# One more FFN pair as a Strassen group, half of the first weight sums added by transfers, and one pass of the down projection per block

## The chip, the core and the metric

The kernel runs on one core of one Trainium2 chip. The metric is the device time of one execution in microseconds (us), the median of several runs. PE is the matmul engine (TensorE), DVE is VectorE, ACT is ScalarE, POOL is GpSimd and SP is SyncE, which here only issues transfers. PEld in a view is the loading of a matmul's stationary operand, which overlaps the matmul before it.

## What is computed

One block of a streaming encoder on 256 frames of width 2048, all in float32: a half-step SwiGLU FFN, two token mixers side by side (chunked attention and retention), a second half-step FFN and a last norm.

```python
def swiglu_ffn(x, w_gate, w_up, w_down):
    return (jax.nn.silu(x @ w_gate) * (x @ w_up)) @ w_down

x = x + 0.5 * swiglu_ffn(rmsnorm(x, norm_ffn1_g[l]), ffn1_w_gate[l], ffn1_w_up[l], ffn1_w_down[l])
h = rmsnorm(x, norm_mix_g[l]); proj = h @ w_in[l]     # 2048 x 11264, then attention, retention, gates
x = x + merged @ w_out[l]
x = x + 0.5 * swiglu_ffn(rmsnorm(x, norm_ffn2_g[l]), ffn2_w_gate[l], ffn2_w_up[l], ffn2_w_down[l])
return rmsnorm(x, norm_final_g)
```

The hidden width of an FFN is 5632, which is 11 blocks of 512 columns. Each block needs a pair of products, x by 512 columns of w_gate and x by the same 512 columns of w_up, and then 512 rows of w_down.

## The kernel before

**Products.** A float32 operand is split into hi (rounded to the matmul's float32r type, a cast on ACT, line L126) and lo (the rest, a subtraction on DVE, line L127). A product is three matmuls (`three`, lines L137, L138, L140): hi by hi, lo of the activations by hi of the weights, hi of the activations by lo of the weights. The activations stand transposed, 128 by 128, and the weights run past them 512 columns at a time, so every matmul of the list is 128x512.

**Steps.** The whole program is one list of steps. A step uses one weight tile of 2 by 128 rows by 512 columns (512 KB). A standard step serves both 128-frame tiles with it: 12 matmuls. `run` walks the list; for each step it issues the steps' loads (SP queue, 5 buffers `raw`), prepares weights up to four steps ahead (`prep`, 4 buffers each of hi and lo) and then issues the step's matmuls. What a job's end hands out (copies, gates, norms) is put some steps later by `later`. Every engine works its own instructions in the order in which they were issued.

**Strassen groups.** `Strassen` computes the pair of products of one block with 7 half-size products in place of 8. Its weight quarters are: k, the upper half of the w_up rows (tiles `z..k`, four of them, jc 0 to 3), x, the upper half of the w_gate rows (tiles `z..x`), and the two lower halves, which arrive as `raw` tiles. k and x are loaded by POOL's queue, eight transfers of 512 KB into a ring of 30 tiles that activations and gates use too. A group (named z and a step number, such as z243) has four phases of half-size steps, 6 matmuls each; `r` steps use a loaded quarter and `s` steps use a sum:

- phase 0: `00r 01r 00s 02r 01s 03r 02s 03s`. The r steps split k and then add k to x on DVE (`first`, line L528); the s steps split that sum.
- phase 1: the r steps split a raw tile and add it to x (L583); the s steps split x, then x minus k goes to k (L570) and a POOL transfer with `accum_op=add` adds another quarter of w_up to x straight from memory (`third`, line L571).
- phase 2: raw tiles and the new k. Phase 3: the four x tiles.

Products run on sums of the activations that were prepared once. At the end of phases, `end` copies and combines the partial results.

**Which pairs.** Of 11 blocks per FFN, nine are groups and two (`PLAIN = (9, 10)`) are done as standard jobs of 8 steps for gate and 8 for up. The five wide pairs of the mixers' input projection are groups too.

**Down.** `down` multiplies the hidden blocks by w_down in passes: a pass takes one or two blocks and runs four jobs, one for each 512 columns of the result. All passes but the last add to x in place: a job's two PSUM banks are seeded with twice x (ACT, L775), the products are added, and half of the bank is copied back (ACT, L778). Passes are `((9, 0), (1, 2), (10, 3), (4, 5), (6,), (7,), (8,))`.

**Weaving.** `weave` mixes the standard steps (plain pairs and down) into the groups: after each pair of group steps it earns `rate * SHARE[i]`, and a standard step goes in when enough is earned and its inputs are at hand. The last pass and six steps more are kept for the end of the FFN.

Of the kernel before, what the change touches and what calls it, by code (L numbers as in the profile page):

```python
# [72 lines left out]
def block_kernel(ctx: ExitStack, tc: tile.TileContext, x, g1, w1g, w1u, w1d, gm, w_in, rel, woa, wor, wo,  # L73
# [439 lines left out]
    class Strassen:  # L513
# [1 line left out]

        def __init__(self, norm, w1, col1, w2, col2, evict):
# [15 lines left out]
        def loads(self):  # L534


            def go(tiles, i, jc):
                tiles[jc] = apool.tile([P, KC, NB], F32, tag="act", name=f"{self.name}{'kx'[i]}{jc}")
                nc.gpsimd.dma_start(tiles[jc], chunk(self.w[i], self.rows(0, jc), self.col[i]))

            return [
                lambda tiles=tiles, i=i, jc=jc: go(tiles, i, jc)
                for jc in range(HALF_K // KC) for i, tiles in enumerate((self.kept, self.x))
            ]

        def steps(self):

# [9 lines left out]
        def step(self, phase, jc, of_sum):  # L557
            made = {}
            name = f"{self.name}{phase}{jc}{'rs'[of_sum]}"
            n = HALF_K // KC  # L560

            def load():
                made["raw"] = weights_tile(f"raw{name}")
                i = 2 - phase
                fetch(made["raw"], self.w[i], self.rows(1, jc), self.col[i])

            def third():

# [24 lines left out]
            bank, form, fresh, closing = {  # L593
# [4 lines left out]
            }[phase, of_sum]  # L598
# [68 lines left out]

        return done

    def weave(jobs, apart, groups, lead, start=None):  # L670


        queue = [(job, k) for job in jobs for k in range(0, job.nk, KC)]
# [14 lines left out]

        for _ in range(lead):
            next_standard()  # L690
        rate = (len(queue) - apart) / (len(groups) * sum(SHARE))
        credit = 0.0
        first = len(steps) - 8
        for n, (b, make) in enumerate(groups.items()):
            group = make()
            loads = group.loads()
            if start is not None and n == 0:
                loads[0] = lambda load=loads[0]: [start(), load()]
            kept.extend((first + i if n == 0 else 0, fn) for i, fn in enumerate(loads))
            for i, part in enumerate(group.steps()):  # L700
                steps.extend(part)
                credit += rate * SHARE[i]
                if i + 1 == len(SHARE):
# [8 lines left out]
    def ffn(name, norm, wg, wu, wd, after, start=None):  # L712
# [10 lines left out]
        def plain(b):  # L723
            gates = {}

            wait = GATE_WAIT if start is not None and b == PLAIN[0] else 0

            def gate_done(acc):
                def go():
# [20 lines left out]
        def paired(b):  # L750
            got = {}

            def evict(t, side, r):
                if side == 1:
                    nc.scalar.activation(r, r, AF.Silu)
                    got[t] = r
                    return
                nc.vector.scalar_tensor_tensor(got[t], r, norm.scale(t), got[t], op0=ALU.mult, op1=ALU.mult)
                if t == 1:
                    later(4, lambda: put_mid(b, got))  # L760

            return Strassen(norm, wu, b * NB, wg, b * NB, evict)

        def down(blocks, last):

# [30 lines left out]
        groups = {b: (lambda b=b: paired(b)) for b in range(nblocks) if b not in PLAIN}  # L796
        weave(jobs, len(downs[PASSES[-1]]) * len(PASSES[-1]) * 4 // KC + HELD, groups, LEAD, start)


    n1 = Norm("n1", gains[:, 0, :], True)  # L800
# [221 lines left out]
    def gates(col1, col2, func, dsts):  # L1022
# [22 lines left out]
        0, groups, MIX_LEAD,  # L1045
    )
    mixed = len(steps)
    add([proj(VR + NB, nat_done("vr", 1, AF.Copy))])
# [209 lines left out]
```

## Time and profile before

| | |
|---|---|
| runs | 2064.11 us median of 3 (2062.82 to 2065.65) |
| profiled execution | span 2061.4 us, the only time it has |
| PE, DVE, ACT, POOL busy | 2045.3, 1754.4, 1402.9, 273.3 us |
| transfers | 473.28 MB, 230 GB/s on average |
| first FFN, mixers, second FFN | up to about 700 us, to about 1360 us, to the end |
| one group of the first FFN (z243) with what is woven in | 454.35 to 520.52 us |

The median of the runs is 2.7 us above the span of the profiled execution. A view by windows gives, for each stretch, the busy time of each engine with the count of its instructions, the granted clock of PE and the mean busy share of the 16 DMA engines (a share a little above 1 comes from packets that end outside of the window). A matmul's own duration in the rows (0.39 us) includes the pipeline; the distance between two starts is what one costs.

### The profile page before, as it was taken

What the parts mean: (1) busy time and instruction counts of PE and PEld (TensorE: products, weight loads), DVE (VectorE), ACT (ScalarE), POOL (GpSimd) and SP (SyncE); (2) the same over time, 40 slices, a digit from 0 to 9 for tenths busy, and PEclk for the clock granted to TensorE, in tenths of its full rate; (3) what the DMA queues carried; (4) which work ended last, traced back from release to release, by engine and by line L of the source; (5) the groups of instructions that cost most, each with busy time, mean ns of one, the idle gap of its engine ahead of it and who ended that gap; (6) DMA issues with size and microseconds to landing.
All of it is one profiled execution on the core that took longest, in us unless ns stands there. A gap on an engine that the chain in (4) does not pass through costs nothing.

```text
span 2061.4 us, 26148 instructions
## 1 busy us (share of the span) xinstructions
PE 2045.3 (99%) x9256; PEld 1691.9 (82%) x9256; DVE 1754.4 (85%) x1824; ACT 1402.9 (68%) x1732; POOL 273.3 (13%) x322
## 2 busy tenths in 40 slices
PE   9999999999999999999999999999999999999998
PEld 7788888888888888888888888888888878888886
DVE  7998899899997799899966667568989988998986
ACT  7677667777777767776665434556776677677785
POOL 1111211122111110122100000010122012110200
PEclk9999999999999999999999999999999999999999
DMA  8776876788678777788775645575787668876873
GB/s 308 207 225 230 269 227 207 239 264 258 191 231 258 240 205 251 258 284 260 227 267 175 223 143 187 187 245 170 235 273 234 200 224 273 240 206 233 281 215 133
DMA packets 219315, 473.28 MB, mean 230 GB/s; under 512 B 14816, under 2 KB 15568, under 8 KB 219184
## 3 DMA queue, kind: packets, MB, share of 16 engines
q1 hardware_dynamic: 161088, 309.89, 44.7%
q0 software_dynamic: 54752, 155.88, 27.9%
q10 hardware_dynamic: 3344, 5.84, 0.8%
q8 instruction: 72, 1.18, 0.2%
q14 instruction: 59, 0.48, 0.1%
HBM read 462.65 MB, written 8.91 MB: 229 GB/s over the span
## 4 chain that ended last, share of the span: by engine, by line
PE 93%; DVE 3%; DMA 2%; ACT 1%; issue 1%; SPq 0%; DVEq 0%; POOLq 0%; POOL 0%; ACTq 0%
PE acc L140 17%; PE acc L137 17%; PE acc L138 17%; DMA raw<-in_ffn_w_down_dram 2%; DVE lo L127 1%; ACT hi L126 0%; PE z684a L140 0%; PE z380a L137 0%; PE z953a L138 0%; PE z684a L138 0%; PE z418a L137 0%; PE z723a L138 0%; PE z380a L140 0%; PE z281a L138 0%; PE z723a L137 0%
## 5 line engine op out<-in xcount | busy, mean ns | idle before, releaser
L127 DVE TENSOR_TENSOR lo<-raw,hi 128x1024 fp32r<-128x1024 f32 x399 | 487.1, 1224 | 179.1 <-ACT hi L126 174.3
L126 ACT CAST hi<-raw 128x1024 fp32r<-128x1024 f32 x399 | 417.7, 1050 | 226.8 <-PE acc L138 143.7
L775 ACT ACTIVATE acc<-xall 128x512 f32<-128x512 f32 x96 | 57.5, 599 | 8.0 <-DVE f1g L742 3.6
L778 ACT ACTIVATE xall<-acc 128x512 f32<-128x512 f32 x96 | 56.6, 589 | 9.2 <-PE acc L140 7.4
L137 PE MATMUL acc<-hi,mgh 128*128 128x512 f32 x128 | 50.2, 392 | 0.0
L138 PE MATMUL acc<-hi,mgl 128*128 128x512 f32 x128 | 49.9, 390 | 0.0
L137 PE MATMUL acc<-hi,nma01h 128*128 128x512 f32 x96 | 38.7, 403 | 0.0
L137 PE MATMUL acc<-hi,nma00h 128*128 128x512 f32 x96 | 38.6, 402 | 0.0
L138 PE MATMUL acc<-hi,nma00l 128*128 128x512 f32 x96 | 37.5, 391 | 0.0
L137 PE MATMUL acc<-hi,nma10h 128*128 128x512 f32 x96 | 37.5, 391 | 0.0
L138 PE MATMUL acc<-hi,nma01l 128*128 128x512 f32 x96 | 37.5, 390 | 0.0
L138 PE MATMUL acc<-hi,nma11l 128*128 128x512 f32 x96 | 37.5, 390 | 0.0
L137 PE MATMUL acc<-hi,nma11h 128*128 128x512 f32 x96 | 37.4, 390 | 0.0
L138 PE MATMUL acc<-hi,nma10l 128*128 128x512 f32 x96 | 37.4, 390 | 0.0
L140 PE MATMUL acc<-lo,mgh 128*128 128x512 f32 x128 | 35.6, 390 | 0.0
L140 PE MATMUL acc<-lo,nma01h 128*128 128x512 f32 x96 | 29.6, 390 | 0.0
L140 PE MATMUL acc<-lo,nma00h 128*128 128x512 f32 x96 | 29.6, 390 | 0.0
L140 PE MATMUL acc<-lo,nma11h 128*128 128x512 f32 x96 | 29.6, 390 | 0.0
L140 PE MATMUL acc<-lo,nma10h 128*128 128x512 f32 x96 | 29.6, 390 | 0.0
L140 PEld LDWEIGHTS acc<-lo,mgh 128*128 128x128 f32 x128 | 24.0, 188 | 5.0
L137 PEld LDWEIGHTS acc<-hi,mgh 128*128 128x128 f32 x128 | 24.1, 188 | 4.9
L138 PEld LDWEIGHTS acc<-hi,mgl 128*128 128x128 f32 x128 | 24.1, 188 | 4.8
(6130 smaller groups left out, 6933.7 us busy)
## 6 DMA issues: line engine op xcount, KB each, us to landing
raw<-in_ffn_w_down_dram SPq DMA_DIRECT2D x176, 512.0 KB, 6.1
raw<-in_w_in_dram SPq DMA_DIRECT2D x96, 512.0 KB, 4.7
raw<-in_ffn_w_up_dram SPq DMA_DIRECT2D x32, 512.0 KB, 10.2
raw<-in_w_out_dram SPq DMA_DIRECT2D x32, 512.0 KB, 4.0
raw<-in_ffn_w_gate_dram SPq DMA_DIRECT2D x31, 512.0 KB, 5.9
raw<-in_w_out_att_dram SPq DMA_DIRECT2D x16, 512.0 KB, 4.3
raw<-in_w_out_ret_dram SPq DMA_DIRECT2D x16, 512.0 KB, 4.0
z380x<-in_w_in_dram POOLq DMA_DIRECT2D x8, 512.0 KB, 7.4
```

The source lines that it names most:

```text
L126: nc.scalar.copy(hi, raw)
L127: nc.vector.tensor_sub(lo, raw, hi.bitcast(F32))
L137: nc.tensor.matmul(acc, ahi, whi, start=first, stop=False, **more)
L138: nc.tensor.matmul(acc, alo, whi, start=False, stop=False, **more)
L140: nc.tensor.matmul(acc, ahi, wlo, start=False, stop=last, **more)
L775: nc.scalar.activation(acc, xs[t][:, cols], AF.Copy, scale=2.0)
L778: nc.scalar.activation(xs[t][:, cols], acc, AF.Copy, scale=0.5)
```

## The change

Three things change, in both FFNs; the mixers keep their shares under the name `MIX_SHARE`.

1. Block 9 becomes a group too: ten of eleven pairs are groups, and only block 10 is plain.
2. For two of the four x tiles of each FFN group (`ADDED = (2, 3)`), the sum x + k is no longer made by DVE. After the last of the eight loads, POOL issues two transfers that read k's quarter of w_up from memory again and add it to x. Groups of the mixers keep the sums on DVE.
3. Every pass of down takes a single block: `((10,), (0,), (1,), ... (9,))`. `SHARE` is another table: fewer standard steps in phase 0 and phase 2, more in phase 1.

```diff
-SHARE = (0.85,) * 4 + (1.0,) * 4 + (0.8,) + (0.4,) * 3 + (0.15,) * 4
-PLAIN = (9, 10)
-PASSES = ((9, 0), (1, 2), (10, 3), (4, 5), (6,), (7,), (8,))
+MIX_SHARE = (0.85,) * 4 + (1.0,) * 4 + (0.8,) + (0.4,) * 3 + (0.15,) * 4
+SHARE = (0.7,) * 2 + (0.2,) * 2 + (1.3,) * 4 + (0.3,) * 4 + (0.2,) * 4
+ADDED = (2, 3)
+PLAIN = 10
+PASSES = ((10,),) + tuple((b,) for b in range(10))
...
+            def add_on():
+                for jc in self.added:
+                    nc.gpsimd.dma_start(self.x[jc], chunk(self.w[0], self.rows(0, jc), self.col[0]), accum_op=ALU.add)
...
+            out[-1] = lambda last=out[-1]: [last(), add_on()]
...
                     if phase == 0:
                         made["w"] = split(self.kept[jc], name)
-                        self.first(jc)
+                        if jc not in self.added:
+                            self.first(jc)
...
-            return Strassen(norm, wu, b * NB, wg, b * NB, evict)
+            return Strassen(norm, wu, b * NB, wg, b * NB, evict, ADDED)
...
-        first, second = [plain(b) for b in PLAIN]
-        order = [first, second[:1], downs[PASSES[0]], second[1:]] + [downs[p] for p in PASSES[1:]]
-        jobs = [job for part in order for job in part]
+        jobs = plain(PLAIN) + [job for p in PASSES for job in downs[p]]
```

In the changed kernel these lines stand a little lower: L126 and L127 are L128 and L129, `first` is L531, the loads L542, the added transfers L546, `third` L580, seeding and copying back L785 and L788.

**POOL's queue.** Before, for the group z243: the last of its eight loads, then the four accumulating transfers of phase 1. A name with in_ffn1_w_up is w_up, with w_gate w_gate.

```order
L539 DMA z243k2_3860<-in_ffn1_w_up_dram 128x2x512
L539 DMA z243x2_3873<-in_ffn1_w_gate_dram 128x2x512
L539 DMA z243k3_3887<-in_ffn1_w_up_dram 128x2x512
L539 DMA z243x3_3905<-in_ffn1_w_gate_dram 128x2x512
L571 DMA z243x0_3776<-in_ffn1_w_up_dram 128x2x512
L571 DMA z243x1_3830<-in_ffn1_w_up_dram 128x2x512
L571 DMA z243x2_3873<-in_ffn1_w_up_dram 128x2x512
L571 DMA z243x3_3905<-in_ffn1_w_up_dram 128x2x512
```

After, for z263, the group at the same place:

```order
L542 DMA z263k2_4140<-in_ffn1_w_up_dram 128x2x512
L542 DMA z263x2_4153<-in_ffn1_w_gate_dram 128x2x512
L542 DMA z263k3_4167<-in_ffn1_w_up_dram 128x2x512
L542 DMA z263x3_4185<-in_ffn1_w_gate_dram 128x2x512
L546 DMA z263x2_4153<-in_ffn1_w_up_dram 128x2x512
L546 DMA z263x3_4185<-in_ffn1_w_up_dram 128x2x512
L580 DMA z263x0_4050<-in_ffn1_w_up_dram 128x2x512
L580 DMA z263x1_4104<-in_ffn1_w_up_dram 128x2x512
L580 DMA z263x2_4153<-in_ffn1_w_up_dram 128x2x512
L580 DMA z263x3_4185<-in_ffn1_w_up_dram 128x2x512
```

Two transfers (L546) stand behind the last load. The first waits for the landing of the load of x2, the second for that of x3. In the program before, the load into x3 waits until the tile that it takes over was split in phase 3 of the group ahead (31s); in the changed one the ring of 30 tiles has more free tiles, and that load waits for the split of 21s, in the middle of phase 2. The last group of the second FFN waits for 23s.

**DVE, phase 0.** Before, z243; a name `lo` with a number alone is the split of a standard step:

```order
L127 TENSOR_TENSOR loz24300r_3915<-z243k0_3750,hiz24300r_3914 128x1024
L528 TENSOR_TENSOR z243x0_3776<-z243x0_3776,z243k0_3750 128x1024
L127 TENSOR_TENSOR loz24301r_3927<-z243k1_3818,hiz24301r_3926 128x1024
L528 TENSOR_TENSOR z243x1_3830<-z243x1_3830,z243k1_3818 128x1024
L127 TENSOR_TENSOR loz24300s_3938<-z243x0_3776,hiz24300s_3937 128x1024
L127 TENSOR_TENSOR loz24302r_3948<-z243k2_3860,hiz24302r_3947 128x1024
L528 TENSOR_TENSOR z243x2_3873<-z243x2_3873,z243k2_3860 128x1024
L758 SCALAR_TENSOR_TENSOR z205c22_3881<-z205a_3401,n1rstd_88,z205c22_3881 128x512
L127 TENSOR_TENSOR lo247_3961<-raw247_3726,hi247_3960 128x1024
L127 TENSOR_TENSOR loz24301s_3973<-z243x1_3830,hiz24301s_3972 128x1024
L127 TENSOR_TENSOR loz24303r_3984<-z243k3_3887,hiz24303r_3983 128x1024
L528 TENSOR_TENSOR z243x3_3905<-z243x3_3905,z243k3_3887 128x1024
```

After, z263:

```order
L129 TENSOR_TENSOR loz26300r_4197<-z263k0_4024,hiz26300r_4196 128x1024
L531 TENSOR_TENSOR z263x0_4050<-z263x0_4050,z263k0_4024 128x1024
L129 TENSOR_TENSOR loz26301r_4209<-z263k1_4092,hiz26301r_4208 128x1024
L531 TENSOR_TENSOR z263x1_4104<-z263x1_4104,z263k1_4092 128x1024
L129 TENSOR_TENSOR loz26300s_4220<-z263x0_4050,hiz26300s_4219 128x1024
L129 TENSOR_TENSOR loz26302r_4230<-z263k2_4140,hiz26302r_4229 128x1024
L768 SCALAR_TENSOR_TENSOR z227c22_4161<-z227a_3706,n1rstd_88,z227c22_4161 128x512
L129 TENSOR_TENSOR lo267_4242<-raw267_4000,hi267_4241 128x1024
L129 TENSOR_TENSOR loz26301s_4254<-z263x1_4104,hiz26301s_4253 128x1024
L129 TENSOR_TENSOR loz26303r_4265<-z263k3_4167,hiz26303r_4264 128x1024
L129 TENSOR_TENSOR loz26302s_4275<-z263x2_4153,hiz26302s_4274 128x1024
```

The sums into x2 and x3 (L528 before) are gone, and one split of a standard step has left this stretch.

**ACT, the end of phase 1 and the start of phase 2.** Before, z243, from the change of one down job to the next (L775 seeds, L778 copies back) on:

```order
L775 ACTIVATE acc28_0_4206<-xall_77 128x512
L778 ACTIVATE xall_77<-acc26_0_4028 128x512
L775 ACTIVATE acc29_1_4209<-xall_77 128x512
L778 ACTIVATE xall_77<-acc27_1_4031 128x512
L126 CAST hiz24312s_4212<-z243x2_3873 128x1024
L126 CAST hiz24313s_4224<-z243x3_3905 128x1024
L126 CAST hi265_4236<-raw265_4106 128x1024
L126 CAST hiz24320r_4254<-rawz24320r_4137 128x1024
L126 CAST hiz24321r_4266<-rawz24321r_4149 128x1024
L629 ACTIVATE z243c12_4278<-z243a_3953,n1minus_89 128x512
L126 CAST hi268_4280<-raw268_4180 128x1024
L126 CAST hiz24320s_4298<-z243k0_3750 128x1024
```

After, z263:

```order
L785 ACTIVATE acc56_0_4450<-xall_77 128x512
L788 ACTIVATE xall_77<-acc54_0_4306 128x512
L785 ACTIVATE acc57_1_4453<-xall_77 128x512
L788 ACTIVATE xall_77<-acc55_1_4309 128x512
L128 CAST hiz26312s_4456<-z263x2_4153 128x1024
L128 CAST hiz26313s_4468<-z263x3_4185 128x1024
L128 CAST hi283_4480<-raw283_4354 128x1024
L128 CAST hiz26320r_4498<-rawz26320r_4381 128x1024
L128 CAST hiz26321r_4510<-rawz26321r_4393 128x1024
L639 ACTIVATE z263c12_4522<-z263a_4234,n1minus_89 128x512
L128 CAST hi286_4524<-raw286_4424 128x1024
L785 ACTIVATE acc58_0_4542<-xall_77 128x512
```

A down job now has two steps and not four, so the next four instructions of seeding and copying back come eight instructions later; before, none stands in the rows shown. In all there are 64 more seeds and 64 more copies back.

More of the change, by code (lines that the diff above doesn't have):

```diff
@@ L513, in block_kernel, with __init__ @@
     class Strassen:
-        def __init__(self, norm, w1, col1, w2, col2, evict):
+        def __init__(self, norm, w1, col1, w2, col2, evict, added=()):
+            self.added = added
             self.norm, self.w, self.col, self.evict = norm, (w1, w2), (col1, col2), evict
@@ L539, in go @@
                 nc.gpsimd.dma_start(tiles[jc], chunk(self.w[i], self.rows(0, jc), self.col[i]))
-            return [
+            def add_on():
+                for jc in self.added:
+                    nc.gpsimd.dma_start(self.x[jc], chunk(self.w[0], self.rows(0, jc), self.col[0]), accum_op=ALU.add)
+            out = [
                 lambda tiles=tiles, i=i, jc=jc: go(tiles, i, jc)
@@ L544, in loads @@
             ]
+            out[-1] = lambda last=out[-1]: [last(), add_on()]
+            return out
         def steps(self):
@@ L668, in x_updated, with weave @@
         return done
-    def weave(jobs, apart, groups, lead, start=None):
+    def weave(jobs, apart, groups, lead, share, start=None):
         queue = [(job, k) for job in jobs for k in range(0, job.nk, KC)]
@@ L690, in weave @@
             next_standard()
-        rate = (len(queue) - apart) / (len(groups) * sum(SHARE))
+        rate = (len(queue) - apart) / (len(groups) * sum(share))
         credit = 0.0
@@ L701, in weave @@
                 steps.extend(part)
-                credit += rate * SHARE[i]
-                if i + 1 == len(SHARE):
+                credit += rate * share[i]
+                if i + 1 == len(share):
                     at_hand[b] = len(steps) + 7
@@ L724, in plain @@
             gates = {}
-            wait = GATE_WAIT if start is not None and b == PLAIN[0] else 0
+            wait = GATE_WAIT if start is not None and b == PLAIN else 0
             def gate_done(acc):
@@ L790, in ffn @@
         downs = {blocks: down(blocks, blocks is PASSES[-1]) for blocks in PASSES}
-        first, second = [plain(b) for b in PLAIN]
-        order = [first, second[:1], downs[PASSES[0]], second[1:]] + [downs[p] for p in PASSES[1:]]
-        jobs = [job for part in order for job in part]
+        jobs = plain(PLAIN) + [job for p in PASSES for job in downs[p]]
         for job, follow in zip(jobs, jobs[1:]):
             job.next = follow
-        groups = {b: (lambda b=b: paired(b)) for b in range(nblocks) if b not in PLAIN}
-        weave(jobs, len(downs[PASSES[-1]]) * len(PASSES[-1]) * 4 // KC + HELD, groups, LEAD, start)
+        groups = {b: (lambda b=b: paired(b)) for b in range(nblocks) if b != PLAIN}
+        weave(jobs, len(downs[PASSES[-1]]) * len(PASSES[-1]) * 4 // KC + HELD, groups, LEAD, SHARE, start)
     n1 = Norm("n1", gains[:, 0, :], True)
@@ L1044, in block_kernel @@
         + [proj(VR, nat_done("vr", 0, AF.Copy), both)],
-        0, groups, MIX_LEAD,
+        0, groups, MIX_LEAD, MIX_SHARE,
     )
```

## The prediction

> **What bounds the kernel now.** I read the page first: busy times, the queues, the chain.
>
> ```profile
> span 2061.4 us, 26148 instructions
> PE 2045.3 (99%) x9256; PEld 1691.9 (82%) x9256; DVE 1754.4 (85%) x1824; ACT 1402.9 (68%) x1732; POOL 273.3 (13%) x322
> q1 hardware_dynamic: 161088, 309.89, 44.7%
> q0 software_dynamic: 54752, 155.88, 27.9%
> PE 93%; DVE 3%; DMA 2%; ACT 1%; issue 1%; SPq 0%; DVEq 0%; POOLq 0%; POOL 0%; ACTq 0%
> ```
>
> PE is busy 99% of the span and carries 93% of the chain that ended last, so about 16 us (2061.4 - 2045.3) are all that a better order could win. The clock allows nothing more:
>
> ```profile
> core 0: 2061.4 us, clock 0.999
> ```
>
> The price of a matmul comes from single rows, the first matmuls of two Strassen steps that follow each other in the group z128:
>
> ```profile
> 316.56 0.39 PE L137 MATMUL z128a<-hiz12832s,n1a11h 128*128 128x512 f32 x1
> 317.92 0.39 PE L137 MATMUL z128a<-hiz12833s,n1a11h 128*128 128x512 f32 x1
> ```
>
> Their starts are 1.36 us apart, with six matmuls between: 0.2267 us each. A Strassen step costs PE 1.36 us, a standard one (12 matmuls) 2.72 us.
>
> Then the view by windows, for the four phases of the group z243 with the standard steps woven in, to see which engine is close behind PE where:
>
> ```profile
> core 0: us, PE busy (x) PEld busy (x) DVE busy (x) ACT busy (x) POOL busy (x), PEclk, DMA share, GB/s
> 454.35:474.28 19.93, 19.93 (x93) 16.60 (x92) 19.93 (x20) 16.53 (x21) 0.00 (x0) 1.00 0.30 89
> 474.28:496.04 21.76, 21.76 (x97) 18.02 (x96) 21.73 (x20) 15.24 (x18) 6.90 (x8) 1.00 0.94 244
> 496.04:515.08 19.04, 19.04 (x85) 15.77 (x84) 14.09 (x14) 13.84 (x18) 3.79 (x6) 1.00 1.03 350
> 515.08:520.50 5.42, 5.42 (x25) 4.51 (x24) 5.05 (x6) 4.58 (x6) 0.00 (x0) 1.00 1.02 377
> ```
>
> PE is full in all four. DVE is full as well in phases 0 and 1 (41.66 of 41.69 us), with room only in phase 2 (4.95 us). The DMA engines lie idle in phase 0 (share 0.30) and are full in phases 1 to 3. So a group has two near-bounds: DVE in its first half, the transfers in its second.
>
> **The change, part by part.**
>
> *Matmuls.* A plain pair is 16 standard steps, 192 matmuls. A group is 7 products of four steps, 28 steps of 6, 168 matmuls. Twice 24 are saved: 48 x 0.2267 = **-10.9 us** on an engine with no slack. Nothing else changes PE's work: down has the same steps however its passes are cut.
>
> *DVE.* The costs of one:
>
> ```profile
> L127 DVE TENSOR_TENSOR lo<-raw,hi 128x1024 fp32r<-128x1024 f32 x399 | 487.1, 1224 | 179.1 <-ACT hi L126 174.3
> L528 DVE TENSOR_TENSOR z243x<-z243x,z243k x4: 1218/1221/1222, 452.3 to 463.2; 128x1024 f32<-128x1024 f32 x4
> ```
>
> Per FFN the new group has 28 splits for the 16 of the pair (+12) and 12 sums; the ten groups lose 20 sums: 4 instructions of 1.22 us more, for both FFNs some 10 us of 1754 on an engine that is 85% busy. Where they fall matters more. Fewer standard steps are left for more groups: by the changed list z263 has 8 (1, 4, 2 and 1 in its phases), where z243 had 10 (3, 4, 3, 0), so a group shrinks from 66.15 us (520.50 - 454.35) to 28 x 1.36 + 8 x 2.72 = 59.8. Phases 0 and 1 lose two splits and two sums, and DVE there 4 x 1.22: 41.66 - 4.9 = 36.8 us. PE loses two standard steps, and takes 16 x 1.36 + 5 x 2.72 = 35.4. DVE is 1.4 us over in the first half, and gets back its slack in phases 2 and 3 (4.95 + 0.37 us in z243). Weights are prepared four steps ahead, at least 4 x 1.36 = 5.4 us, so a lag of 1.4 that is paid back in each group reaches nobody: 0. Such a cover has been drawn on before, in phase 1 of z684:
>
> ```profile
> 1425.02:1445.26 20.24, 20.24 (x93) 16.40 (x92) 20.24 (x21) 13.56 (x15) 5.37 (x6) 1.00 0.84 204
> ```
>
> DVE had no idle moment there and PE lost none. If the cover were gone, it would be 1.4 x 18 = 25 us (the groups but the first of each FFN).
>
> *The first group of each FFN.* Its phase 1 holds only two standard steps now: 8 x 1.36 + 2 x 2.72 = 16.3 us of PE. DVE has two large instructions in each of the eight Strassen steps and a split in the others, 18 x 1.22 = 22.0, or 5.7 over. The four steps' lead less the cast that it begins with (5.4 - 1.05) covers 4.4, a step's own length up to 1.0 more. Left are 0.3 to 1.3 us; I take the middle, 0.8 for each FFN: **+1.6**.
>
> *ACT.* Single-block passes seed and copy back twice as often:
>
> ```profile
> L775 ACT ACTIVATE acc<-xall 128x512 f32<-128x512 f32 x96 | 57.5, 599 | 8.0 <-DVE f1g L742 3.6
> L778 ACT ACTIVATE xall<-acc 128x512 f32<-128x512 f32 x96 | 56.6, 589 | 9.2 <-PE acc L140 7.4
> L126 ACT CAST hi<-raw 128x1024 fp32r<-128x1024 f32 x399 | 417.7, 1050 | 226.8 <-PE acc L138 143.7
> ...
> 585.00:630.00 45.00, 45.00 (x205) 37.35 (x204) 43.01 (x40) 35.73 (x47) 5.39 (x6) 1.00 0.66 189
> ```
>
> 64 x 0.599 + 64 x 0.589 + 24 casts of 1.05 = 101 us more on an engine with 658 idle (2061.4 - 1402.9), 73% then. The last row is a stretch that already runs a pass of one block, over 45 us: ACT at 79% and PE with no gap. Cost 0; without that room, a job's change would add up to the 1.2 us of a pair of seeds.
>
> *Transfers.* 64 more on POOL's queue (24 for two more groups, 40 added sums), 33.6 MB; 16 raw loads less on SP's, 8.4 MB. Their price is in the queues' rows for 476 to 500 us, where POOL's queue holds accumulating transfers and SP's plain loads:
>
> ```profile
> q0 software_dynamic: 996, 1.94, 48.4%
> q1 hardware_dynamic: 1974, 3.81, 46.7%
> ```
>
> Half a megabyte (0.524 MB) took the 16 engines 0.524 / 1.94 x 0.484 x 24 = 3.1 us as an accumulating transfer and 1.54 us as a load. A group moved 51.5 us of transfers in its 66.15 (0.30 x 19.93 + 0.94 x 21.76 + 1.03 x 19.04 + 1.02 x 5.42); two sums more and two raw loads less make 51.5 + 6.2 - 3.1 = 54.6 in 59.8, or 91%. The sums' share fits into phase 0, about 13.6 us long (8 x 1.36 + 2.72) with 6.0 us of transfers now (0.30 x 19.93): 12.2 of 13.6. The rest stays as full as it was. Who is late when the engines are full is seen in the raw loads, in a quiet window and in one behind a phase 1, with the median time to landing last:
>
> ```profile
> raw<-in_ffn_w_down_dram SPq DMA_DIRECT2D x4, 512.0 KB, 3.8
> raw<-in_ffn_w_down_dram SPq DMA_DIRECT2D x5, 512.0 KB, 11.3
> ```
>
> 3.8 us against 11.3, though they stand on another queue than POOL's. I read "full" here from the engines' share. The Trainium skill, page "Perfetto Trace Analysis", section "Identifying the Most-Contended Engine", says to judge transfers by the use of the HBM and not by occupancy, which 16 engines make misleading. By that measure phase 1 (244 GB/s, against 377 in phase 3) is a third empty, raw loads have room, and the sum would be that of rival 4; by share (0.94) it is full. The trace's 11.3 us speak for the share, since the engines spend twice the time on each accumulated byte.
>
> What such a delay costs is in the chain, at the worst place of the run:
>
> ```profile
> 1650.82 11.20 DMA raw<-in_ffn_w_down_dram
> ...
> 1662.11 1.04 ACT L126 CAST hi<-raw 128x1024 fp32r<-128x1024 f32 x1 [2.54 <-PE z800b L140]
> 1663.20 0.50 PE L137 MATMUL acc<-hi,f2a1h 128*128 128x512 f32 x1 [1.17 <-ACT hi L126]
> ```
>
> A load of 11.2 us held PE up by 1.17. There are few such places, and all of PE's waits for these casts sum to 1.3 us:
>
> ```profile
> PE acc L137 <- ACT hi L126: 1.3, 2, 1.2
> ```
>
> Bounds: -1.3 us, if all of these go, and 20 x 1.17 = +23, if every group had one. The added transfers are issued behind the last load and land where phase 0 has free engines, so I take 0, nearer to the first.
>
> *The added sums' own wait.* x2 and x3 are first split at 02s and 03s, steps 7 and 8 of phase 0. The load of x3 waits for the split of 21s (it ended at 503.4 in z243), and the next group begins at 520.52, 17 us behind:
>
> ```profile
> 502.16 1.22 DVE L127 TENSOR_TENSOR loz24321s<-z243k,hiz24321s 128x1024 fp32r<-128x1024 f32 x1
> 520.52 0.39 PE L137 MATMUL z281a<-hiz28100r,n1a00h 128*128 128x512 f32 x1
> ...
> DMA to landing us min/median/max: 5.9/7.9/12.5
> ```
>
> In the changed order 14.5 to 18 us of steps lie between these two. The three numbers are the landing times of POOL's transfers for z243's x tiles. Load and sum behind one another take 2 x 7.9 = 15.8 us at the median, 25 at worst: they end 1.3 us behind the group's start, or 10.5. The cast of 03s is due 7 x 1.36 - 1.05 = 8.4 us behind it where no standard step comes first, else 11.2. At the median there are 7 us to spare; at worst 2 us lack, in the four groups without a standard step. I take 0, with +8 as its end. POOL's queue holds nothing behind these two until the third sums of phase 1.
>
> **The sum.** 2061.4 - 10.9 + 1.6 + 0 = 2052.1 us of span. The median of the runs stands 2.7 above the profiled execution (2064.11), so the runs should show **2055 us**, 0.44% less. A measurement of this kernel tells a difference from no change from about 0.2% on, 4.1 us: 2060.0 to 2068.2 is "same".
>
> **Rivals.**
>
> 1. *The transfers become the bound* (the other side). 91% of a group is a mean; if the table's four standard steps in phase 1, with their raw loads, meet the accumulating transfers, a raw load lands late in each group, as at 1662.11. 20 x 1.17 = 23 us against 10.9 saved: 2064.1 - 10.9 + 23 = 2076. It decides from 0.55 us per group (10.9 / 20) on. For it: shares of 0.94 to 1.03 in phases 1 to 3. Against: the added bytes fall into phase 0.
> 2. *DVE holds phases 0 and 1.* 1.4 us in 18 groups: 2064.1 - 10.9 + 25 = 2078; with half of it hidden, 2066, no difference to be measured. For it: 41.66 of 41.69 us. Against: z684's phase 1, and 5.3 us of slack behind.
> 3. *The added sum is late.* 2 us in four groups: 2055 + 8 = 2063, same; in all 20, 2095.
> 4. *The raw waits vanish as well*, with the engines emptier in phases 1 to 3 than I reckon: 2055 - 1.3 - 1.6 = 2052.
>
> **How the numbers follow.** The likeliest 0.60, rival 4 0.13: both faster. Rival 1 in full 0.09, at half its size (2065) 0.04; rival 2 in full 0.03, half hidden 0.03; rival 3 small 0.05, large 0.03. Faster: 0.73; same: 0.04 + 0.03 + 0.05 = 0.12; slower: 0.09 + 0.03 + 0.03 = 0.15. The range runs from 2049, rival 4 with another 3 us of PE's idle time gone, to 2069, which takes in the halves of rivals 1 and 2 and the small case of 3, and leaves out 0.15. The likeliest alone: 2050 to 2060.
>
> **What would show it.** In the profile after: 48 matmuls of 128x512 fewer; groups of about 60 us; q0 near 189 MB and 36%, q1 near 301; ACT at 73%, seeds and copies x160. Step by step: the added transfers (L546) land before the casts of 02s and 03s, and PE waits for no `hi` there; DVE is full in phases 0 and 1 and idle some us in 2; PE waits for casts of `raw` stay near 1 us in all. It is wrong if PE idles more than half a us in each group, with raw loads behind it (rival 1), with DVE never idle from 00r to 13s (rival 2), or with the casts of 02s and 03s waiting for POOL's queue (rival 3).

## The result and the profile after

The changed kernel takes 2077.93 us (median of 4 runs, 2077.83 to 2079.74) where the kernel before takes 2063.47: 0.72% slower, ratio 1.0072 (95% interval 1.0058 to 1.0087). The forecast was 2055. The page of the changed kernel, with the lines that answer to those of before:

```profile
span 2078.0 us, 26280 instructions
PE 2047.3 (99%) x9208; PEld 1680.7 (81%) x9208; DVE 1768.2 (85%) x1836; ACT 1490.7 (72%) x1892; POOL 342.3 (16%) x386
q1 hardware_dynamic: 156736, 301.50, 42.9%
q0 software_dynamic: 70112, 189.44, 35.7%
L788 ACT ACTIVATE xall<-acc 128x512 f32<-128x512 f32 x160 | 94.5, 591 | 17.6 <-PE acc L142 13.1
L785 ACT ACTIVATE acc<-xall 128x512 f32<-128x512 f32 x160 | 95.8, 599 | 15.2 <-DVE f1g L752 7.0
```

The work is what the diff says: 48 matmuls fewer, q0 at 189 MB, 160 seeds and 160 copies. PE looks as full as before, 99%, with 48 matmuls fewer and 2 us more of busy time, because a matmul's row (0.39 us or more) is longer than the distance between two starts (0.2267) and so covers a part of each wait. (The Trainium skill, page "Perfetto Trace Analysis", section "Identifying the Most-Contended Engine", calls the busy share of matmuls no good measure, since they are pipelined, and names the share of the weight loads beside the flops reached. The trace agrees: that share went from 82.1%, 1691.9 of 2061.4, to 80.9%, 1680.7 of 2078.0, and 1.2% of the span are 25 us.) What shows the waits one by one is the distance between starts. Summed over all 128x512 matmuls, what lies above 0.2267 us each is 23.0 us before and 48.3 after: 25.4 us more, against 10.9 saved. The rest of the 16.6 us between the two spans is 2.2 us around transposes (the profiled execution, 2079.74, is the slowest of the four).

The four phases of z263 by windows, to be laid beside those of z243:

```profile
core 0: us, PE busy (x) PEld busy (x) DVE busy (x) ACT busy (x) POOL busy (x), PEclk, DMA share, GB/s
482.06:498.53 16.47, 15.07 (x70) 11.75 (x68) 16.47 (x17) 14.64 (x20) 0.00 (x0) 1.00 0.36 80
498.53:520.46 21.93, 21.93 (x96) 18.12 (x97) 21.93 (x21) 15.92 (x19) 6.10 (x7) 1.00 0.95 241
520.46:536.78 16.32, 16.32 (x73) 13.51 (x72) 13.61 (x13) 13.36 (x17) 4.52 (x7) 1.00 1.05 356
536.78:544.94 8.16, 8.16 (x37) 6.76 (x36) 5.78 (x7) 5.65 (x8) 2.43 (x2) 1.00 1.06 352
```

Phases 0 and 1 take 38.4 us, not 35.4 and not DVE's 36.8, and DVE has no idle moment in them. The 35.4 of the forecast counts steps alone and leaves out the eight transposes in phase 0 (0.8 us); counted from z243's window, as DVE's 36.8 was, PE's own work is 41.69 - 2 x 2.72 = 36.25. The rest of the 38.4 is nearly all two waits, 0.90 us at 00s and 1.05 at 10r. DVE itself does the list of these phases without a gap in 37.0 us (480.73 to 517.76), as forecast, and the instructions beyond that in these two windows prepare phase 2. Its idle time stays behind, in phases 2 and 3 (5.1 us), where little can be done with it, since weights are prepared at most four steps ahead.

The waits of PE (total, times, longest; of eight rows at 10r and seven at 00s one each stands here):

```profile
PE acc L139 <- ACT hi L128: 2.0, 3, 1.3
PE acc L142 <- DVE lo L129: 1.7, 5, 0.6
...
PE z263c L139 <- ACT z263s L636: 0.8, 1, 0.8
...
PE z263c L142 <- DVE loz26300s L129: 0.6, 1, 0.6
```

By the distances between starts, these places hold (of the 48.3 us; before the change the first three hold less than 1 us together):

| place | us | where |
|---|---|---|
| 10r behind 03s | 8.4 | eight groups, 1.05 each |
| 00s, the split is late | 5.8 | eight groups, 0.2 to 0.9 each |
| standard steps behind 12r, 13r and 13s, the split is late | 4.9 | six groups |
| the first group of each FFN | 7.0 | 2.7 before |
| casts of `raw` | 3.8 | 3.0 before |
| 03s of z1019, the added sum is late | 1.1 | one |

Two of them in rows. At the end of phase 0, PE and ACT:

```profile
497.13 0.61 PE L142 MATMUL z263c<-loz26303s,n1s5h 128*128 128x512 f32 x2
498.53 0.50 PE L139 MATMUL z263c<-hiz26310r,n1s3h 128*128 128x512 f32 x1 [0.78 <-ACT z263s L636]
...
497.79 0.69 ACT L636 ACTIVATE z263s<-z263c,n1minus 128x512 f32<-128x512 f32 x1 [0.23 <-PE z263c L142]
```

10r goes on in the PSUM bank c that 03s has just finished, and ACT copies the bank out in between. In the list before, a standard step always stands between 03s and 10r and covers the copy; the new table of shares leaves it out in eight groups. And at the turn from one group to the next, ACT and DVE:

```profile
471.69 0.59 ACT L785 ACTIVATE acc<-xall 128x512 f32<-128x512 f32 x1
472.22 0.58 ACT L788 ACTIVATE xall<-acc 128x512 f32<-128x512 f32 x1
472.83 0.60 ACT L785 ACTIVATE acc<-xall 128x512 f32<-128x512 f32 x1
473.37 0.58 ACT L788 ACTIVATE xall<-acc 128x512 f32<-128x512 f32 x1
473.85 1.04 ACT L128 CAST hiz22730s<-z227x 128x1024 fp32r<-128x1024 f32 x1
...
474.92 1.22 DVE L129 TENSOR_TENSOR loz22730s<-z227x,hiz22730s 128x1024 fp32r<-128x1024 f32 x1 [1.88 <-ACT hiz22730s L128]
...
485.27 1.22 DVE L129 TENSOR_TENSOR loz26300s<-z263x,hiz26300s 128x1024 fp32r<-128x1024 f32 x1
...
486.54 0.74 PE L142 MATMUL z263c<-loz26300s,n1s5h 128*128 128x512 f32 x2 [0.62 <-DVE loz26300s L129]
```

The change of a down job (2.2 us of ACT) stands in front of the cast of 30s; DVE idles 1.88 us for it, then works without a gap for ten instructions, and is late at 00s. A table of how early the splits are shows it for all FFN groups: the median time from the end of a split to the first matmul that uses it, worked out from the rows (us):

```
        before  after  no_seeds_no_copies  no_first_sums  sums_on_dve
33s      2.89    1.52       2.93               1.52          1.52
00r      2.77    2.13       3.05               2.31          2.13
01r      1.86    1.22       2.13               2.27          1.22
00s      2.17    0.31       1.71               2.58          0.31
02s      1.88    2.91       3.34               3.72          0.91
03s      2.11    1.96       2.47               2.61          0.34
10r      3.18    3.32       3.36               3.36          2.03
13s      1.34    1.64       1.73               1.69          0.88
```

No median in it reaches 4 us. At 00s it was 2.2 us before, and 0.3 after. The loss stands already at 33s, at the end of the group ahead (2.89 before, 1.52 after), and it is gone there when the seeds and copies of down are left out (2.93).

### The profile page after: what moved, and what is told of

Its sections match the earlier page's. It is cut to its first block, busy times and chain, and to the rows that moved or that the text cites. A ratio compares the mean times of both kernels' runs of the same rounds, so it can differ in the third digit from the quotient of the medians.

```text
span 2078.0 us, 26280 instructions
## 1 busy us (share of the span) xinstructions
PE 2047.3 (99%) x9208; PEld 1680.7 (81%) x9208; DVE 1768.2 (85%) x1836; ACT 1490.7 (72%) x1892; POOL 342.3 (16%) x386
## 5 line engine op out<-in xcount | busy, mean ns | idle before, releaser
L129 DVE TENSOR_TENSOR lo<-raw,hi 128x1024 fp32r<-128x1024 f32 x367 | 447.8, 1224 | 163.4 <-ACT hi L128 161.1
L128 ACT CAST hi<-raw 128x1024 fp32r<-128x1024 f32 x367 | 384.0, 1050 | 206.4 <-PE acc L140 140.0
L788 ACT ACTIVATE xall<-acc 128x512 f32<-128x512 f32 x160 | 94.5, 591 | 17.6 <-PE acc L142 13.1
L785 ACT ACTIVATE acc<-xall 128x512 f32<-128x512 f32 x160 | 95.8, 599 | 15.2 <-DVE f1g L752 7.0
```

Source lines behind the costliest of these rows:

```text
L128: nc.scalar.copy(hi, raw)
L129: nc.vector.tensor_sub(lo, raw, hi.bitcast(F32))
L785: nc.scalar.activation(acc, xs[t][:, cols], AF.Copy, scale=2.0)
L788: nc.scalar.activation(xs[t][:, cols], acc, AF.Copy, scale=0.5)
```

## The experiments

All ratios are to the kernel before, run on the same chip; it measured 2062.29 to 2063.47 us in the different sets of runs, so variants from different sets can be told apart from 1 to 2 us on. The theories: waits at 10r are a matter of the copy alone, or of DVE; late splits come from DVE's own work, from ACT's, or from transfers.

**The copy at 10r.** A standard step forced in behind 03s:

```diff
-                turn = i + 1 == 3 * (HALF_K // KC)
+                turn = i + 1 in (HALF_K // KC, 3 * (HALF_K // KC))
```

> The changed kernel with one edit: a standard step is forced in behind 03s in every FFN group, as the list already does behind phase 2. In eight groups (z84, z120, z263, z299 and their four fellows of the second FFN) this moves one standard step from behind 11r to behind 03s; nothing else moves. Theory of the copy: in these eight, PE waits 1.05 us at 10r for ACT's copy out of the bank c; a step of 2.72 us covers it, so 8 x 1.05 = 8.4 us go: 2077.9 - 8.4 = 2069.5. Theory of DVE: the wait at 10r is only where PE pays for a DVE that is behind in phases 0 and 1; DVE gets no time to catch up, and the same eight groups wait some 0.9 us for the split of the standard step in front of 13s, as z48, z227, z732 and z911 do that have this order already: 2077 (within 2 us of 2077.9).

2077.03 us (in brackets here and below the ratio and its 95% interval: 1.0066, 1.0052 to 1.0079). All eight waits at 10r are gone from the trace, and 6.4 us stand in their place at the standard steps before 13s (4.9 became 11.3). The copy was the place where PE waited and not what the time hangs on: without the wait there, the splits are late a few steps on.

**The transfers, and DVE's sums.** First without the added transfers, then without the other two sums as well:

```diff
-            out[-1] = lambda last=out[-1]: [last(), add_on()]
...
-                        if jc not in self.added:
-                            self.first(jc)
```

> The changed kernel without the 40 added transfers: x2 and x3 are split without k (that part of the computation is left out), so 21 MB less on POOL's queue, and DVE, ACT and PE do the same work as in the changed kernel. Theory of the transfers: raw loads land in time, ACT and DVE are no longer pushed back behind them, and the waits at 00s (5.8 us), at the standard steps before 13s (4.9), for raw casts (3.8) and at z1019's 03s (1.1) go: about 2077.9 - 15 = 2063. Theory of DVE: only the raw waits shrink and z1019's goes, 2 to 3 us: about 2075. The eight waits at 10r (8.4) stay under both.

> As the kernel without the added transfers, and the first sums of x0 and x1 on DVE are left out as well (that part of the computation is left out): DVE has two instructions of 1.22 us less in phase 0 of each of the 20 groups. Theory of DVE: its lateness in phases 0 and 1 was 1.4 us a group, 2.44 us less remove it: the waits at 00s and at the standard steps before 13s go whole (10.7 us), also most of the first groups' 4.3: about 10 to 13 us below the kernel without the added transfers. Theory of the transfers: that kernel has already won this; no more than 2 us below it. The eight waits at 10r stay.

2075.74 us (1.0061, 1.0048 to 1.0073) and 2068.31 (1.0026, 1.0016 to 1.0036). The transfers cost about 2 us (the two intervals overlap, the single times do not), as the theory of DVE had it; 40 DVE instructions (49 us of DVE) cost 7.4, less than the 10 to 13 expected. The waits at 00s go to nothing, those before 13s only from 4.9 to 3.4. The converse, all four sums as transfers (`ADDED = (0, 1, 2, 3)`), and none (`ADDED = ()`):

> The changed kernel with all four first sums as added transfers, not two: 40 more of 3.1 us on the DMA engines, 40 DVE instructions of 1.22 us less in phase 0. Theory of DVE: the waits at 00s and before 13s go (10.7 us), and some of the first groups': about 2065 to 2068 if the transfers find room. Theory of the transfers: another 6.2 us of the engines in each group (up to 97% of 59.8 us) push raw loads and x3's sum later: 2 us or more per group, 2100 or above.

> The changed kernel with the added sums undone: all four first sums on DVE, ten groups, single passes and the new table. Theory of DVE: 2.44 us more of DVE in phase 0 of each group, where it is already late, come out at PE in full or nearly: 20 x 1 to 2.4 = 20 to 48 us slower, 2098 to 2126. Rival (transfers): 2 us faster, as when the transfers were left out.

2153.23 us (1.0436, 1.0422 to 1.0450) and 2105.39 (1.0206, 1.0193 to 1.0219). With four, the sum of x0 comes too late for 00s, the third step, since it is issued behind the last load; 49.9 us are lost there by the distances between starts, the most in these two groups:

```profile
PE z1019c L139 <- ACT hiz101900s L128: 6.9, 1, 6.9
PE z227c L139 <- ACT hiz22700s L128: 5.0, 1, 5.0
```

With none, 27.5 us are lost, within the 20 to 48 expected: beside the 48 matmuls, the two added sums are the part of the change that pays.

**ACT.** The seeds and copies of down left out (both functions empty, and the first matmul of a job starts its bank):

> The changed kernel without the 160 seeds and 160 copies back of the down jobs (the additions of the down passes are left out): ACT has 190 us less to do. Theory of ACT: DVE is late at 00s and before 13s because ACT's four instructions at each change of a down job (2.2 us) stand in front of the casts that DVE waits for; these waits go (10.7 us): about 2067, and the waits at 10r stay. Theory of DVE: its own work is what is late, and ACT has room: within 2 us of 2077.9.

2068.35 us (1.0022, 1.0013 to 1.0032): 9.6 us faster. The waits at 00s are gone, as the theory of ACT had it; the eight at 10r stay, but those before 13s only go from 4.9 to 4.2. ACT, 72% busy, holds PE up by its place ahead of DVE, in the turn from group to group.

**The order.** Two other tables for the changed kernel, the first also with the sums on DVE, and the table of the kernel before:

```diff
+SHARE = (1.0, 0.0, 0.0) + (1.0,) * 5 + (0.0, 0.0, 1.0, 1.0) + (0.0,) * 4    # spread
+SHARE = (0.0,) * 3 + (1.0,) * 5 + (0.0, 0.0, 1.0, 1.0) + (0.0,) * 3 + (1.0,)    # late_single
+                credit = min(credit, 0.9)    # late_single, in weave
+SHARE = MIX_SHARE    # old_shares
```

> The changed kernel with another table of shares: every group but the first of each FFN has a standard step behind 03s and four in phase 1, two at the end of phase 2, and the eighth behind 01r or 33s. z156 and z191 stand nearly so in the changed kernel, and PE waits nowhere in them. Theory of DVE: what counts is that five standard steps stand around phase 1 (1.5 us of room for DVE in each); then the waits at 10r (8.4 us), at 00s (5.8) and before 13s (4.9) go, and the first groups' 4 and some raw waits stay: about 2060, down to 0.2% below the kernel before. Theory of the transfers: five standard steps in a row of phase 1 draw more raw loads into the time of the accumulating transfers; waits for raw casts of 0.5 us a group come instead: about 2070.

> The same table, and no added transfers: all four first sums on DVE as before the change. Against the kernel with the table alone DVE has two instructions of 1.22 us more in phase 0 of 20 groups, and the DMA engines 40 transfers less. Theory of DVE: it needs then 97% of a group and the waits come back, 0.5 to 2 us a group: 10 to 40 us slower than the table alone. Theory of the transfers: 2 us faster, as when the transfers were left out.

> The changed kernel with the table of shares of the kernel before: each group has a standard step behind 03s, but two or three in phase 0 and only two or three inside phase 1. Theory of the copy at 10r: the eight waits go: 2069.5. Theory of DVE: a standard step less in phase 1 leaves DVE 1.5 us short there, more than is won at 10r; waits before 13s or at 20r of 0.5 to 1.5 us in most groups: 2075 to 2085.

> The changed kernel with a third table: in every group of both FFNs no standard step inside phase 0, one behind 03s, four in phase 1, two at the end of phase 2 and one behind 33s (and no more than 0.9 of a step saved up). Passes of a single block, so the down job changes every second standard step. Theory of ACT and DVE together: PE waits where the casts and splits, prepared at most four steps ahead, come late; a step behind 33s gives 2.7 us in front of 00r where the sums begin. The waits at 00s, 10r and half of the first groups' go (16 us), but the changes of the down job stay where they are, and the waits before 13s stay (5): 2064 to 2068. Theory of DVE alone: what counts is that five standard steps stand around phase 1: 2060.

2074.22 us (1.0049, 1.0035 to 1.0063), 2102.51 (1.0185, 1.0169 to 1.0201), 2085.67 (1.0109, 1.0096 to 1.0123) and 2071.05 (1.0040, 1.0027 to 1.0053). The expectation for the first was missed by 14 us: with five standard steps around phase 1 the waits move in part into phase 0 (3.5 us at the steps behind 01r and 2.6 behind 03s), and 6.3 stay around 13s. The sums on DVE cost 28.3 us under this table, as the theory of DVE had it. The third table was missed by 3 to 11: the waits at 00s and 10r all but go, those around 13s grow from 4.9 to about 10. No table brings the waits to nothing; each moves them, and the best wins 6.9 us. The old table is 7.7 us worse than the new one, near what the theory of DVE said, so the new table is not what costs.

**Passes of two.** Under the third table, with `PASSES = ((10,), (0, 1), (2, 3), (4, 5), (6, 7), (8,), (9,))`, with the added sums and without:

> The same table of shares, but passes of two blocks where the kernel before had them, ((10,), (0, 1), (2, 3), (4, 5), (6, 7), (8,), (9,)): 64 seeds and 64 copies back less, as before the change, and the second group has four standard steps fewer, others one more. Theory of ACT: the four instructions of a job's change (2.2 us) eat the casts' lead; with half as many the waits before 13s and the rest go: 4 to 8 us below the kernel with single passes, about 2058. Theory of DVE: ACT's work has room, no difference above 2 us, or slower because of the second group.

> As the one with passes of two blocks, but all four first sums on DVE as before the change (no added transfers). Against it DVE has 2.44 us more in phase 0 of each of 20 groups. With the table that was spread and single passes this cost 28 us. Theory of DVE: that price again, 20 to 30 us. Theory of ACT: half of it, since DVE is late only behind late casts: 5 to 15 us.

2089.22 us (1.0123, 1.0107 to 1.0138) and 2092.96 (1.0145, 1.0131 to 1.0159): the numbers of both theories of ACT were missed, and that of the price on DVE too (3.7 us); only "slower because of the second group" came true. A pass of two waits for its second block, the second group stands with four standard steps, and in the short time to the next group the added sums land late (19.6 us of PE's waits stand at 02s and 03s). ACT's rows in z80:

```profile
172.52 1.04 ACT L128 CAST hiz8002s<-z80x 128x1024 fp32r<-128x1024 f32 x1 [3.81 <-DMA z80x<-in_ffn_w_up_dram]
175.73 1.04 ACT L128 CAST hiz8003s<-z80x 128x1024 fp32r<-128x1024 f32 x1 [2.16 <-DMA z80x<-in_ffn_w_up_dram]
```

This pair tells nothing of ACT's price.

**Each part alone in the kernel before.** Single passes; the added sums; the tenth group:

```diff
-PASSES = ((9, 0), (1, 2), (10, 3), (4, 5), (6,), (7,), (8,))
+PASSES = ((9,), (0,), (1,), (10,)) + tuple((b,) for b in range(2, 9))    # singles_before
+ADDED = (2, 3)    # added_before, with the two issues of the change
+PLAIN = 10; PASSES = ((10, 0), (1, 2), (3, 4), (5, 6), (7,), (8,), (9,))    # tenth_alone
```

> The kernel before with one part of the change alone: down in passes of one block each, ((9,), (0,), (1,), (10,), (2,), ... (8,)); nine groups, two plain blocks, the sums on DVE and the old table of shares stay. Theory of ACT: 48 seeds and 48 copies back more in 18 groups come in front of casts; PE starts to wait at the same places as in the changed kernel: 3 to 8 us slower, 2067 to 2071. Theory of the standard steps: with ten of them in a group the lead absorbs ACT's four instructions: within 2 us of 2063.3.

> The kernel before with the second part alone: the first sums of x2 and x3 as added transfers (36 of them, 36 DVE instructions less). Theory of the standard steps: PE waits for DVE hardly anywhere in that kernel, so there is nothing to win: 2062 to 2064. Theory of the transfers: the sums of x3 or the raw loads behind them come late, 0.3 to 1 us in each of 18 groups: 2069 to 2080.

> The third part alone: ten groups and one plain block, with the sums on DVE, the old table of shares and passes of two blocks ((10, 0), (1, 2), (3, 4), (5, 6), (7,), (8,), (9,)). The plain block no longer fills the time until the blocks of a pass are at hand, so the standard steps bunch in every second group. Theory of the standard steps: this part takes 16 PE-heavy steps out of each FFN and puts a group with 40 large DVE instructions in; DVE has then 97% to do in the groups and PE waits 2 us a group: 2085 to 2105, slower than the whole change, whose other parts win back some of it. Rival: the saved matmuls pay here, and the other parts lose it: about 2055.

2068.95 us (1.0026, 1.0017 to 1.0035), 2061.19 (0.9994, 0.9985 to 1.0002) and 2127.72 (1.0314, 1.0300 to 1.0328), against 2062.29. Single passes cost 5 to 7 us (by the ratio and by the medians) already where ten standard steps stand in a group. The median lead at 33s falls there from 2.89 to 2.36 us. But the profiled execution (2065.79, one of the two quickest of ten) has only 2.6 us more of span, 0.9 around the 128x512 matmuls and 1.7 around transposes, and late splits at 00s in one group alone, so where the rest of the price arises is not shown. The added sums win nothing that can be told from noise there, where PE waits for a DVE split three times in the view (0.8 us). The tenth group alone is the worst by far, beyond what was expected, but not purely for its own sake: with passes of two, standard steps bunch, and raw loads and the bank a at 30s are waited for too (18.5 us at the steps behind 23r and 10.7 at 30s, by the distances):

```profile
ACT hi L128 <- DMA raw<-in_ffn_w_down_dram: 47.7, 30, 3.7
...
PE z84a L139 <- ACT z84c L650: 0.9, 1, 0.9
```

A cleaner figure is the changed kernel with its sums on DVE (2105.39): tenth group, single passes and the new table together, 42 us slower than before.

**Half a change of job.** The second bank's seed and copy issued a step later, under the third table:

```diff
-        if follow is not None:
-            begin(1)
+        def second():
+            if follow is not None:
+                begin(1)
+            if job.evict is not None:
+                job.evict(job.acc[1], 1)
...
         if job.evict is not None:
-            job.evict(job.acc[1], 1)
+            later(1, second)
+        else:
+            second()
```

> The kernel with the third table and single passes (2071.05), where a change of the down job is cut in two: the seed and the copy back of the second bank are issued a step later, so that one cast comes between. Same work on every engine. Theory of the place: what hurts is that 2.2 us of ACT stand in one piece in front of a cast; halves cost less: 2 to 4 us faster, 2067 to 2069. Theory of the amount: ACT and DVE have too little room in sum, no difference above 1.5 us.

2068.77 us (1.0029, 1.0017 to 1.0040), 2.3 less than with the table alone, and the quickest whole version with ten groups; the two intervals overlap, so the two theories are not told apart. It does not beat the kernel before.

**The lead.** Five split buffers have room only with three raw ones; a control has four and three:

```diff
-RAW_BUFS = 5
-SPLIT_BUFS = 4
+RAW_BUFS = 3
+SPLIT_BUFS = 5
```

> The changed kernel with three raw buffers in place of five: a control for the run with five split buffers, which has no room for more. Raw loads are issued later; waits for raw casts grow. By the loads' median of 6.6 us against two steps less of lead (2.7 to 5.4 us): some 0.5 to 3 us for each group, 2088 to 2138.

> The control with five buffers each of hi and lo, so that weights are prepared five steps ahead and not four. Theory of the lead: DVE and ACT have time enough in a whole group (93% and 81%), and it is the short lead that lets PE wait in phases 0 and 1; a step more (1.36 us at least) covers waits of 0.2 to 1.3 us: at least 10 us faster than the control. Theory of the amount: DVE and ACT are full for longer than any lead reaches: within 3 us of the control.

2345.52 us (1.1363, 1.1348 to 1.1378) and 2314.57 (1.1213, 1.1190 to 1.1236). The control was far beyond its range, and ACT waits for down's raw loads ten times as long as in the changed kernel (23.6 us), 246.0 and 245.4 us; the control's row:

```profile
ACT hi L128 <- DMA raw<-in_ffn_w_down_dram: 246.0, 70, 9.6
```

The 31 us between them are on the side of the lead, but in a kernel bound by its loads. By the distances, and without the first group of each FFN, the fifth buffer takes the waits at 00s from 6.7 to 0.7 us and those around 13s from 53 to 30, while those at 10r grow from 8.4 to 23. Whether it would cure the changed kernel stays open.

## Why the prediction was wrong

- **Matmuls, -10.9: right.** 48 fewer, at the same distance.
- **DVE, 0: this step failed.** The working had 36.8 us of DVE beside 35.4 of PE and called a lag of 1.4 us covered, because slack follows in phases 2 and 3. The size of the lag was not what failed: 37.0 of DVE were measured, and PE's side, with the transposes that the working left out, was 36.25, so the lag was even smaller. The cover failed. The slack is there (5.1 us) and does not help: each turn from group to group is a stretch of its own, from 30s to 13s, and the lead at 00s was 0.31 us, not 5.4. The four steps' lead is the most that the buffers allow, not what the engines had in hand; the kernel before had 1.3 to 3.2 us of it. z684's phase 1, the precedent, is that of the first group of its FFN: in the phase 0 ahead DVE was busy for only 18.94 of 21.76 us, so the group came to 10r with 4.74 us of lead, and at 13s it had 0.05 left. It showed that a whole lead can be spent, not that one is there in each group. With the waits at 10r, which in this kernel stand in for late splits, this is 8.4 + 5.8 + 4.9 = 19 us of the 25.4.
- **ACT, 0: failed too.** Idle share was the wrong measure. Four instructions at each second standard step delay casts, and DVE behind them; leaving them all out wins 9.6 us, and making more of them costs 5 to 7 in the kernel before. These overlap with the 19 above: the same late splits, seen from the engine ahead. The precedent of 585 to 630 us had three standard steps in phase 0 of its group.
- **The first groups, +1.6: 4.3 measured**, since waits come behind phase 1 as well, which was not in the sum: 1.8 us at 20r and 1.6 at the standard step behind 21r, which needs the low half of the plain block's result from DVE.
- **Transfers, 0: held, nearly.** Leaving the added ones out wins about 2 us, raw casts are waited for 0.8 us more, and the added sum is late once, in the last group, 1.1. Their cover is bare: a short group ahead (z80 with passes of two) takes it away. Rival 1 did not happen.
- **Rival 2** gave 2078 in full, and the time came out there, which is in part luck: its 1.4 us in each of 18 groups were not what was measured, and waits of the first groups and of raw casts are in the measured sum. The mechanism is only in part the one it named: DVE alone did not explain the trace, ACT's place ahead of it did the rest, and its chance of 0.03 rested on a precedent instead of on the lead in the rows.
- **Not seen:** the wait at 10r. The changed list was read for the number of standard steps in each phase and not for what stands behind 03s.

Shown is that the added sums win (27.5 us undone), that transfers cost little, and that ACT's and DVE's work from the turn of the groups to 13s is what PE waits for. That the tenth group makes the time short, by taking two standard steps with room for DVE out of each group, is argued from the runs with single parts and not shown: its own price was not had without bunched steps or single passes.

## What to carry to other kernels

When an engine feeds another through a few buffers, check the slack over the stretch that the buffers span, not over the whole period: read the lead of each product from the rows, end of the producer to start of the consumer, and spend no more than the smallest. An in-order engine with 28% idle time still delays what is queued behind a burst. Work that trades a bound engine's instructions for another's moves the bound, and the order that covered a copy or a late cast goes with the steps that are traded away.

## What the hardware did that was not expected

A short wait halved PE's clock. In the kernel with passes of two, PE waited 2.07 us (a distance of 2.29) and, six matmuls later, 1.39 (1.62); the matmuls that followed came 0.427 us apart for 5 us. The windows around it, with the granted clock in the third column from the end, the last one within the second wait:

```profile
170.00:176.00 6.00, 3.63 (x14) 2.04 (x12) 1.45 (x2) 1.31 (x2) 0.37 (x1) 0.96 0.86 148
176.00:182.00 6.00, 5.17 (x12) 4.11 (x13) 5.19 (x6) 6.00 (x9) 0.00 (x0) 0.50 0.06 16
182.00:188.00 6.00, 6.00 (x27) 4.91 (x27) 6.00 (x6) 3.79 (x4) 0.00 (x0) 0.98 0.76 231
...
175.48:176.80 1.32, 0.13 (x1) 0.00 (x0) 0.00 (x0) 1.07 (x2) 0.00 (x0) 0.50 0.00 0
```

The clock was low as the second wait began, so the first was enough. In the run with the tenth group alone, a single wait of 2.06 us did the same; the wait and what followed:

```profile
1546.56:1548.62 2.06, 0.17 (x1) 0.00 (x0) 0.01 (x1) 1.09 (x2) 0.00 (x0) 1.00 1.04 388
1548.97:1552.38 3.41, 3.41 (x10) 2.59 (x9) 3.13 (x3) 2.46 (x3) 0.72 (x1) 0.50 1.02 380
```

The length of the wait alone does not decide: two waits of 1.92 and 1.94 us in the same run cost no clock, nor did one of 3.48 in the run with five split buffers. What decides stays open.

The Trainium skill, page "TensorE: Matmul & The Clock Gate", section "HAM oscillation — how this bites in real kernels", gives as the rule that no idle gap be longer than about 3.4 us. Here 2.06 us were enough; the measurement decides. In the changed kernel itself the longest wait was 1.43 us, and its clock is 0.999.
